# Hybrid decoder trunk on one core: the shared-sum adds placed behind the next step, the loads at pair ends redistributed, and six seven-product steps in the last pair

## The chip, the cores and the metric

The kernel runs on one core of one Trainium2 chip. The metric is device time in microseconds (us) of one execution; lower is better. Before the change three executions took 1211.99, 1211.93 and 1210.82 us, median 1211.93.

## What is computed

One decoder layer on 272 positions (16 meta tokens and 256 tokens) of width 2048: retention heads and mLSTM heads share an input projection `w_in` and an output projection `w_out`; a gated feed-forward network with a causal convolution of width 3 follows; all in float32.

```python
u  = rmsnorm(h, norm_ffn)
up = causal_dwconv(u @ w_up, ffn_conv_w, ffn_conv_b)     # w_up: 2048 x 11264
gate, val = jnp.split(up, [FFN_DIM], axis=-1)            # FFN_DIM 5632
h  = h + (jax.nn.silu(gate) * val) @ w_down              # w_down: 5632 x 2048
return rmsnorm(h, norm_final)[:, N_META:]
```

The change touches the last line but one (the down-projection) and, in small things, how weight tiles are loaded everywhere.

## The kernel before

**Precision.** A product in float32 is made of three matmuls. Each weight tile is loaded raw, ScalarE copies it to a rounded type (`whi`), VectorE subtracts that from the raw tile (`wlo`), and TensorE adds hi by hi, lo-activation by hi, and hi-activation by `wlo` in PSUM (L141, L143, L150 to L153; in the down-projection L768, L770, L821 to L824, L846 to L849). `whi` and `wlo` have five buffers each.

**Raw tiles.** `raw_home` gives them from two names, `wraw0` and `wraw1`, two buffers each. `load_raw` counts loads and takes the sides in the rhythm 0, 0, 1, 1; a tile's load waits until the reader of the tile that last had its buffer is done. Nearly all loads are issued by SyncE (SP), whose queue is in order: a load that waits holds up those behind it. DMAs that accumulate are issued by GpSimd (POOL), also in order.

**The feed-forward part** runs in two halves of the hidden width. In each, an up-projection (88 half-tile loads `in_wu`) is followed by a down-projection into 4 column blocks of 512, taken as two pairs, `b = 0` and `b = 2`. Each pair walks through 11 steps `q` of 256 hidden channels (2 row tiles `tt`, 2 column blocks `j`). A plain step has 24 matmuls of 512 columns. A *seven step* (`seven`, q = 1 to 8) makes seven products instead of eight in Winograd's manner, 21 matmuls: the combined activations `sh`, `sl` are ready, the combined weights are made of a raw tile of four quarters (`left[0]` or `left[1]`, name `hT`, 1 MB), a difference `ta` that VectorE makes (L832, into `wraw`), and a sum `tb` that was formed in DRAM (`Early`: accumulating DMAs during the projections, paced by a count of loads; result `kept`, loaded by POOL, L930). The products that only one block needs go to `cs` (PSUM name `atps`), those that several blocks need to `ps` (`mmps`).

**Ends of pairs.** After the last seven step, `share` gives the shared sums to the residual `hn` with four accumulating DMAs (`onto`, L865). After the last plain step ScalarE copies each `cs` out (L1003) into one of the tiles `x`, which become free when an `onto` has landed, and VectorE adds it to `hn` (L1004), for which the `onto` of the same block must have landed. The first splits of the next pair are placed behind the last copy (`emptied`).

**The last pair** (half 1, `b = 2`, `final`) takes q = 0, 1, 6, 2, 7, 3, 4, 5, 8, 9, 10; the q of `BOTH` (6, 7, 8) are plain there, the others of 1 to 8 seven steps. Its last four plain q (`alone`) do column block 2 first; block 3 follows at the end, row tile 0 in full width, row tile 1 in two halves of 256 columns, so that the final norm of tile 0 (`finish`, L728 to L744) runs beside the products of tile 1. `times_gain` multiplies finished blocks by the final gain on GpSimd (L715) during the seven steps of the last pair.

**Order.** Each engine's order is fixed when the program is built: a scheduler with a model of times places the instructions, under `issue_after` (place behind) and `high_priority`. A change in one place can so change the order in another.

## Time and profile before

| | |
|---|---|
| median of three executions | 1211.93 us |
| profiled execution | 1212.01 us |
| its span, first to last instruction | 1210.2 us (1.8 us around it) |
| PE busy / DVE busy / ACT busy / POOL busy | 99% / 79% / 59% / 21% of the span |
| mean granted TensorE clock | 0.998 |
| memory read and written | 268.59 MB and 42.47 MB, 257 GB/s over the span |

PE is TensorE, DVE VectorE, ACT ScalarE, POOL GpSimd. Down-projection of half 0: 718 to 774 us (`b = 0`) and 774 to 836 us (`b = 2`); of half 1: 1087 to 1145 and 1145 to 1202, then the tail to 1210.2. Busy shares average over stages, so a stage is read by its own window; matmuls are pipelined, so a row of one shows 0.39 us while the next starts 0.23 us later, and a loss is read from start to start.

### The profile page before, as it was taken

Reading aid. Unit: us, or ns where it says so; the run is one execution under the profiler, and the core shown is the slowest. Engines: PE = TensorE matmul, PEld = TensorE weight load, DVE = VectorE, ACT = ScalarE, POOL = GpSimd, SP = SyncE. Lnnn points to the kernel's source line nnn. Section 1 sums busy time; section 2 is a strip of 40 time slices with the busy share of each in tenths; the row PEclk is TensorE's granted clock in tenths of the full one; section 3 lists DMA queues with packets and bytes.
Section 4 is the critical chain, followed back from the end, with each engine's and each line's share of the span. In section 5 each row is a group of like instructions: output and inputs, shape, how many; then the busy total and the mean of one; then the engine's idle time right before and its main releaser. Section 6 shows DMA issues by size and latency. Waiting matters only on the chain.

```text
span 1210.2 us, 23069 instructions
## 1 busy us (share of the span) xinstructions
PE 1198.8 (99%) x8947; PEld 1150.3 (95%) x8947; DVE 951.6 (79%) x1390; ACT 713.4 (59%) x973; POOL 258.7 (21%) x349
## 2 busy tenths in 40 slices
PE   9999999999999999999999999999999999999997
PEld 9999999999999999999999998878999999998786
DVE  8877778766775867788889779897877777778896
ACT  8657746656556556555555557665655555556673
POOL 0100022223231322233132100101133223300132
PEclk9999999999999999999999999999999999999999
DMA  7765677878786977788887757777888778847955
GB/s 278 263 224 159 203 235 210 254 217 238 209 244 208 260 223 222 238 256 227 237 229 224 233 181 261 229 249 228 271 228 252 240 222 237 221 161 265 291 195 183
DMA packets 102366, 278.50 MB, mean 230 GB/s; under 512 B 16432, under 2 KB 20656, under 8 KB 102128
## 3 DMA queue, kind: packets, MB, share of 16 engines
q1 hardware_dynamic: 84016, 239.06, 58.0%
q0 software_dynamic: 17664, 37.11, 17.5%
q8 instruction: 70, 1.15, 0.4%
q10 hardware_dynamic: 576, 0.85, 0.2%
q14 instruction: 40, 0.33, 0.1%
HBM read 268.59 MB, written 42.47 MB: 257 GB/s over the span
## 4 chain that ended last, share of the span: by engine, by line
PE 95%; DMA 2%; DVE 1%; ACT 0%; issue 0%; SPq 0%; DVEq 0%; ACTq 0%
PE mmps L150 25%; PE mmps L153 25%; PE mmps L151 25%; PE atps L821 2%; PE mmps L849 2%; PE atps L822 2%; PE atps L824 2%; PE mmps L846 2%; PE mmps L847 2%; PE atps L846 1%; PE atps L847 1%; PE atps L849 1%; DMA wraw<-in_wu 1%; DVE wlo L770 1%; DMA hT<-kept 1%; PE atps L444 1%
## 5 line engine op out<-in xcount | busy, mean ns | idle before, releaser
L141 ACT CAST whi<-wraw 128x1024 fp32r<-128x1024 f32 x346 | 361.8, 1049 | 334.0 <-PE mmps L151 221.6
L143 DVE TENSOR_TENSOR wlo<-wraw,whi 128x1024 fp32r<-128x1024 f32 x346 | 430.2, 1246 | 79.0 <-ACT whi L141 74.8
L150 PE MATMUL mmps<-uh,whi 128*128 128x258 f32 x1408 | 345.3, 283 | 0.6 <-ACT whi L141 0.6
L151 PE MATMUL mmps<-ul,whi 128*128 128x258 f32 x1408 | 345.0, 281 | 0.0
L151 PEld LDWEIGHTS mmps<-ul,whi 128*128 128x128 f32 x1408 | 266.6, 189 | 0.1
L150 PEld LDWEIGHTS mmps<-uh,whi 128*128 128x128 f32 x1408 | 265.3, 188 | 0.9 <-ACT whi L141 0.8
L150 PE MATMUL mmps<-xh,whi 128*128 128x272 f32 (+2 forms) x864 | 219.7, 287 | 0.0
L151 PE MATMUL mmps<-xl,whi 128*128 128x272 f32 (+2 forms) x864 | 218.2, 285 | 0.0
L153 PE MATMUL mmps<-uh,wlo 128*128 128x258 f32 x1408 | 197.9, 283 | 0.0
L153 PEld LDWEIGHTS mmps<-uh,wlo 128*128 128x128 f32 x1408 | 181.7, 189 | 0.0
L151 PEld LDWEIGHTS mmps<-xl,whi 128*128 128x128 f32 x864 | 162.6, 188 | 0.0
L150 PEld LDWEIGHTS mmps<-xh,whi 128*128 128x128 f32 x864 | 162.5, 188 | 0.1
L210 POOL TENSOR_TENSOR pace<-whi 128x1 f32<-128x1 f32 x87 | 52.2, 600 | 429.9 <-ACT whi L141 411.8
L153 PE MATMUL mmps<-xh,wlo 128*128 128x272 f32 (+2 forms) x864 | 126.8, 285 | 0.0
L153 PEld LDWEIGHTS mmps<-xh,wlo 128*128 128x128 f32 x864 | 114.5, 188 | 0.0
L697 DVE TENSOR_TENSOR cu<-mmps,rstd 128x258 f32<-128x258 f32 x88 | 37.6, 427 | 72.9 <-PE mmps L153 72.2
L770 DVE TENSOR_TENSOR wlo<-hT,whi 128x1024 fp32r<-128x1024 f32 x58 | 69.3, 1218 | 3.5 <-ACT whi L768 3.5
L768 ACT CAST whi<-hT 128x1024 fp32r<-128x1024 f32 x58 | 59.3, 1049 | 15.7 <-DMA hT<-kept 5.3
L768 ACT CAST whi<-wraw 128x1024 fp32r<-128x1024 f32 (+1 forms) x58 | 46.6, 835 | 35.5 <-DVE wraw L832 17.7
L151 PE MATMUL mmps<-mixl,whi 128*128 128x258 f32 x256 | 63.1, 283 | 0.0
L150 PE MATMUL mmps<-mixh,whi 128*128 128x258 f32 x256 | 62.5, 283 | 0.0
L770 DVE TENSOR_TENSOR wlo<-wraw,whi 128x1024 fp32r<-128x1024 f32 (+1 forms) x58 | 53.2, 952 | 1.5 <-ACT whi L768 0.5
(272 smaller groups left out, 1768.3 us busy)
## 6 DMA issues: line engine op xcount, KB each, us to landing
wraw<-in_wu SPq DMA_DIRECT2D x176, 512.0 KB, 4.5
wraw<-in_wi SPq DMA_DIRECT2D x108, 512.0 KB, 4.5
wraw<-in_wo SPq DMA_DIRECT2D x32, 512.0 KB, 5.4
wraw<-in_wd SPq DMA_DIRECT2D x30, 512.0 KB, 5.6
kept<-in_wd SPq DMA_DIRECT2D x29, 512.0 KB, 6.8
kept<-in_wd POOLq DMA_DIRECT2D x58, 256.0 KB, 6.7
hT<-in_wd SPq DMA_DIRECT2D x29, 512.0 KB, 4.9
kept<-kept POOLq DMA_DIRECT2D x29, 256.0 KB, 5.4
```

The lines of the kernel that those rows point to most:

```text
L141: nc.scalar.copy(hi, raw)
L143: nc.vector.tensor_tensor(out=lo, in0=raw, in1=hi.bitcast(F32), op=ALU.subtract)
L150: nc.tensor.matmul(ps, hi[:, k, :], xh(kk), start=kk == first, stop=False)
L151: nc.tensor.matmul(ps, hi[:, k, :], xl(kk), start=False, stop=False)
L153: nc.tensor.matmul(ps, lo[:, k, :], xh(kk), start=False, stop=kk == last)
L210: with tc.issue_after(nc.gpsimd.tensor_tensor(out=pace, in0=x, in1=x, op=ALU.add).ins):
L697: evacuated = nc.vector.tensor_tensor(out=u, in0=ps[:, :NQ], in1=rstd2, op=ALU.mult)
L768: copied = nc.scalar.copy(hi, x)
L770: return copied, nc.vector.tensor_tensor(out=lo, in0=x, in1=hi.bitcast(F32), op=ALU.subtract)
L846: nc.tensor.matmul(o, sh[:, f, m, :], hi[:, i, :], start=begin, stop=False)
L847: nc.tensor.matmul(o, sl[:, f, m, :], hi[:, i, :], start=False, stop=False)
L849: nc.tensor.matmul(o, sh[:, f, m, :], lo[:, i, :], start=False, stop=end)
```

## The change

Six things change. The j = 1 adds of pair `b = 0` (L1004 before, L1019 now) are put into a list `later` and issued behind the last split of the next pair's first seven step. `BOTH` shrinks to q = 7, 8: step 6 of the last pair is a seven step, the order of its steps is 0, 1, 2, 7, 3, 4, 5, 6, 8, 9, 10, one more unit is formed by `Early` (30, not 29, from load 36 on, not 40), and the parked activations `a21` are two tiles, not three. The load of step 2 of pair `b = 2` goes from SP's queue to POOL's, behind `share`. The load of the final gain `gfin` (1 MB) is cut into four, issued during steps 3 to 6 of pair `b = 0` of half 1. The plain loads of the last pair follow its new steps. `loads` starts at 3, which shifts the rhythm of the raw sides by three everywhere.

```diff
@@ -35,7 +35,7 @@
 WARM = 8
-AHEAD, AHEAD_STEP, REST, RESUME = 40, 22, 222, 238
+AHEAD, AHEAD_STEP, REST, RESUME = 36, 22, 222, 238
@@ -114,7 +114,8 @@
     last_load = None
-    loads = paced = 0
+    loads, paced = 3, 0
     def raw_home(shape, side):
         return wpool.tile(shape, F32, name=f"wraw{side}", bufs=2)
@@ -189,7 +190,7 @@
     FAST = [1, 2, 3, 4, 5, 6, 7, 8]
     PLAIN = [q for q in range(NQD) if q not in FAST]
-    BOTH = FAST[-3:]
+    BOTH = FAST[-2:]
     class Early:
@@ -841,7 +842,7 @@
                 lo = wpool.tile([P, 2, 512], F32R, name="wlo", bufs=5)
                 n = len(to)
                 with tc.issue_after(after.ins) if first and after else nullcontext():
-                    copied, _ = split(hi[:, :n, :], lo[:, :n, :], w)
+                    copied, parted = split(hi[:, :n, :], lo[:, :n, :], w)
                 for i, (m, o, begin, _) in enumerate(to):
                     nc.tensor.matmul(o, sh[:, f, m, :], hi[:, i, :], start=begin, stop=False)
                     nc.tensor.matmul(o, sl[:, f, m, :], hi[:, i, :], start=False, stop=False)
@@ -856,6 +857,7 @@
                 with tc.issue_after(reached.ins):
                     for tt, _, c0, c1 in norm:
                         times_gain(tt, c0, c1)
+            return parted
         def block(tt, b):
             return hn[:, tt, b * 512 : (b + 1) * 512]
@@ -893,7 +895,6 @@
             more_cm = pool("more", 2, side="right")
             more = more_cm.__enter__()
             gfin = more.tile([P, DM], F32, name="gfin", bufs=1)
-            nc.gpsimd.dma_start(gfin, io["gfin"])
             junk = more.tile([P, 512], F32, name="junk", bufs=1)
             kept21 = more.tile([P, 2, len(BOTH), P], F32R, name="a21", bufs=1)
             nc.scalar.copy(kept21, left[1].rearrange("p a n -> p (a n)")[:, 0 : 2 * len(BOTH) * P].rearrange("p (s f n) -> p s f n", s=2, n=P))
@@ -901,7 +902,7 @@
         homes, raws = {}, {}
-        begun = shared = None
+        begun = shared = summed = None
         def load(to, src):
             nonlocal begun
@@ -918,23 +919,30 @@
             nonlocal turn
             raw = left[turn]
             turn = 1 - turn
-            load(raw[:, 2:4, :], io["wd7"][b // 2, half * NQD + q][:, 2:4, :])
-            load(raw[:, 1, :], io["wd7"][b // 2, half * NQD + q][:, 1, :])
-            load(raw[:, 0, :], early[b, half * NQD + q].kept[:, 0, :])
+            w = io["wd7"][b // 2, half * NQD + q]
+            parts = ((raw[:, 2:4, :], w[:, 2:4, :]), (raw[:, 1, :], w[:, 1, :]), (raw[:, 0, :], early[b, half * NQD + q].kept[:, 0, :]))
+            for to, src in parts:
+                if (b, q) == (2, 2):
+                    with tc.issue_after(shared.ins):
+                        nc.gpsimd.dma_start(to, src)
+                else:
+                    load(to, src)
             homes[b, q] = raw
         def load_sum(b, q):
+            nonlocal summed
             tb = sums_home[1][:, FAST.index(q) % 2, :][:, None, :]
             with tc.issue_after(shared.ins) if shared else nullcontext():
-                nc.gpsimd.dma_start(tb[:, 0, :], early[b, half * NQD + q].kept[:, 1, :])
+                summed = nc.gpsimd.dma_start(tb[:, 0, :], early[b, half * NQD + q].kept[:, 1, :])
             homes[b, q] = homes[b, q], sums_home[0], tb
         def split_step(raw, to=wpool):
             return split_w(raw, [P, 2, 512], to)
         lag = 4
-        gains = []
+        gains, later = [], []
         emptied = None
         for b in (0, 2):
             cs = {}
@@ -944,7 +952,7 @@
             ps = [mm.tile([P, 512], F32, name="mmps") for _ in range(4)]
             final = half == 1 and b == 2
-            steps = [0, 1, 6, 2, 7, 3, 4, 5, 8, 9, 10] if final else range(NQD)
+            steps = [0, 1, 2, 7, 3, 4, 5, 6, 8, 9, 10] if final else range(NQD)
             fast = [q for q in steps if q in FAST and not (final and q in BOTH)]
             plain = [q for q in steps if q not in fast]
             alone = plain[-lag:] if final else []
@@ -960,7 +968,12 @@
                     due = []
                     if final and q != fast[0]:
                         due, gains = gains[:1], gains[1:]
-                    seven(b, q, cs, ps, q == fast[0], q == fast[-1], emptied, due)
+                    done = seven(b, q, cs, ps, q == fast[0], q == fast[-1], emptied, due)
+                    if q == fast[0]:
+                        with tc.issue_after(done.ins):
+                            while later:
+                                later.pop(0)()
                     if q == fast[-1]:
                         with tc.high_priority() if final else nullcontext():
                             shared = share(ps, b, final)
@@ -972,12 +985,10 @@
                 if final:
                     if q == 0:
-                        load_plain(b, 6, 0)
-                    elif q == 6:
                         load_plain(b, 7, 0, 1)
-                    elif q in (3, 4, 5):
-                        load_plain(b, q + 5, 0 if q < 5 else 1, 1)
-                    if q in (1, 2, 3):
+                    elif q in (4, 5, 6):
+                        load_plain(b, q + 4, 0 if q < 6 else 1, 1)
+                    if q in range(1, 5):
                         load_seven(b, q + 2)
                         load_sum(b, q + 2)
                 else:
@@ -988,6 +999,10 @@
                         load_sum(b, q + 2)
                     if q == 8:
                         load_plain(b, 10, 1)
+                    if (half, b) == (1, 0) and q in range(3, 7):
+                        cols = slice((q - 3) * 512, (q - 2) * 512)
+                        with tc.issue_after(summed.ins):
+                            nc.gpsimd.dma_start(gfin[:, cols], io["gfin"][:, cols])
                     if b == 0:
                         if q == 7:
                             load_seven(2, 1)
@@ -1001,7 +1016,9 @@
                         x = x_tile((4, 3, 1, 0)[2 * j + n])
                         emptied = nc.scalar.copy(x, cs[tt, j])
-                        nc.vector.tensor_tensor(out=block(tt, b + j), in0=block(tt, b + j), in1=x, op=ALU.add)
+                        later.append(lambda to=block(tt, b + j), x=x: nc.vector.tensor_tensor(out=to, in0=to, in1=x, op=ALU.add))
+                        if j == 0 or b == 2:
+                            later.pop(0)()
                         if half == 1:
                             gains.append((tt, b + j, c, c + 512))
                     elif j == 0:
```

VectorE where the last pair begins. L143/L144 split a plain tile, L832/L833 make `ta`, L770/L771 split the parts of a seven step. Before:

```order
L143 TENSOR_TENSOR wlo<-wraw_13666,whi 128x1024
L1004 TENSOR_TENSOR hn<-hn,x_5926 128x512 x4
L770 TENSOR_TENSOR wlo<-hT,whi 128x1024 x2
L770 TENSOR_TENSOR wlo<-wraw_13719,whi 128x1024
L770 TENSOR_TENSOR wlo<-wraw_13720,whi 128x512
L832 TENSOR_TENSOR wraw_13719<-hT 128x1024
L143 TENSOR_TENSOR wlo<-wraw_13755,whi 128x1024
```

The same place now:

```order
L144 TENSOR_TENSOR wlo<-wraw_13675,whi 128x1024
L1019 TENSOR_TENSOR hn<-hn,x_5931 128x512 x2
L771 TENSOR_TENSOR wlo<-hT,whi 128x1024 x2
L771 TENSOR_TENSOR wlo<-wraw_13726,whi 128x1024
L771 TENSOR_TENSOR wlo<-wraw_13727,whi 128x512
L1019 TENSOR_TENSOR hn<-hn,x_5931 128x512 x2
L833 TENSOR_TENSOR wraw_13726<-hT 128x1024
```

Two of the four adds moved behind the splits of step 1; step 2 follows them directly, since step 6 no longer stands between.

SP where the second up-projection begins (`in_wd` with `wraw1`: the two tiles of the last plain step; the `in_wu` tiles are needed in the order of their numbers). Before:

```order
L909 DMA wraw1_9990<-in_wd 128x1024
L909 DMA wraw1_9992<-in_wd 128x1024
L127 DMA wraw0_10071<-in_wu 128x1024
L127 DMA wraw0_10162<-in_wu 128x1024
L127 DMA wraw1_10101<-in_wu 128x1024
L127 DMA wraw1_10132<-in_wu 128x1024
```

The same place now:

```order
L910 DMA wraw1_9995<-in_wd 128x1024
L910 DMA wraw1_9997<-in_wd 128x1024
L128 DMA wraw0_10076<-in_wu 128x1024
L128 DMA wraw0_10106<-in_wu 128x1024
L128 DMA wraw1_10137<-in_wu 128x1024
L128 DMA wraw1_10167<-in_wu 128x1024
```

The tile needed second had the buffer that the last plain step leaves; now it has the other buffer of side 0, and the tile needed third has that one.

PE near the end, from the pair of matmuls that completes row tile 0 (`wlo,mh 128x512 x2`) on. Before:

```order
L824 MATMUL atps<-wlo,mh 128x512 x2
L824 MATMUL atps<-wlo,a_13228 128x256
L824 MATMUL atps<-wlo,sh 128x256
L821 MATMUL atps<-whi,a_13228 128x256
L822 MATMUL atps<-whi,a_13228 128x256
L821 MATMUL atps<-whi,sh 128x256
L822 MATMUL atps<-whi,sl 128x256
```

The same place now:

```order
L825 MATMUL atps<-wlo,mh 128x512 x2
L823 MATMUL atps<-whi,ml 128x256
L825 MATMUL atps<-wlo,mh 128x256 x2
L822 MATMUL atps<-whi,a_13233 128x256
L823 MATMUL atps<-whi,a_13233 128x256
L822 MATMUL atps<-whi,sh 128x256
L823 MATMUL atps<-whi,sl 128x256
```

The pair now stands later among the 256-column matmuls of row tile 1: before, 44 of these followed it to the end of PE's program, now 27.

## Rows read from the trace of the kernel before

**Rows 1.** Chain of waits: shares of the span by engine
```profile
PE 95%; DMA 2%; DVE 1%; ACT 0%; issue 0%; SPq 0%; DVEq 0%; ACTq 0%
```
**Rows 2.** Window of the last pair's seven steps: PE, PEld, DVE, ACT, POOL busy
```profile
1145.00:1184.00 39.00, 39.00 (x169) 31.36 (x169) 36.87 (x33) 26.84 (x35) 12.24 (x11) 1.00 0.61 210
```
**Rows 3.** Timeline of PE, half 1: a seven step's start and the next's
```profile
1092.81 0.39 PE L846 MATMUL atps<-whi,sh 128*128 128x512 f32 x1
...
1097.71 0.39 PE L846 MATMUL atps<-whi,sh 128*128 128x512 f32 x1
```
**Rows 4.** Timeline of PE: where it waits in the down-projections
```profile
814.45 0.63 PE L849 MATMUL mmps<-wlo,sh 128*128 128x512 f32 x2
815.87 0.51 PE L846 MATMUL atps<-whi,sh 128*128 128x512 f32 x1 [0.79 <-ACT whi L768]
...
818.56 0.51 PE L846 MATMUL mmps<-whi,sh 128*128 128x512 f32 x1 [0.16 <-ACT whi L768]
...
836.54 0.39 PE L150 MATMUL mmps<-uh,whi 128*128 128x258 f32 x1 [0.56 <-ACT whi L141]
...
1129.78 0.50 PE L846 MATMUL mmps<-whi,sh 128*128 128x512 f32 x1 [0.18 <-ACT whi L768]
```
**Rows 5.** Chain of waits, the step ahead of 836.54
```profile
826.73 8.63 DMA wraw<-in_wu
```
**Rows 6.** Timeline of DVE, half 0, b = 2
```profile
776.24 0.69 DVE L1004 TENSOR_TENSOR hn<-hn,x 128x512 f32<-128x512 f32 x1 [0.82 <-DMA hn<-x]
778.27 0.69 DVE L1004 TENSOR_TENSOR hn<-hn,x 128x512 f32<-128x512 f32 x1 [1.34 <-DMA hn<-x]
...
816.12 1.23 DVE L832 TENSOR_TENSOR wraw<-hT 128x1024 f32<-128x1024 f32 x1 [1.82 <-DMA hT<-kept]
```
**Rows 7.** Timeline of DVE, last pair
```profile
1148.65 2.36 DVE L770 TENSOR_TENSOR wlo<-hT,whi 128x1024 fp32r<-128x1024 f32 x2
1150.92 1.82 DVE L770 TENSOR_TENSOR wlo<-wraw,whi 128x1024 fp32r<-128x1024 f32 x2
1152.65 1.22 DVE L832 TENSOR_TENSOR wraw<-hT 128x1024 f32<-128x1024 f32 x1
1153.79 2.35 DVE L143 TENSOR_TENSOR wlo<-wraw,whi 128x1024 fp32r<-128x1024 f32 x2
...
1159.59 2.36 DVE L832 TENSOR_TENSOR wraw<-hT 128x1024 f32<-128x1024 f32 x1
...
1180.10 3.44 DVE L143 TENSOR_TENSOR wlo<-wraw,whi 128x1024 fp32r<-128x1024 f32 x2
```
**Rows 8.** Timeline of POOL, last pair
```profile
1159.57 1.30 POOL L715 TENSOR_TENSOR hn<-hn,gfin 128x512 f32<-128x512 f32 x1
```
**Rows 9.** Timeline of ACT, where the last pair begins
```profile
1146.38 2.00 ACT L768 CAST whi<-hT 128x1024 fp32r<-128x1024 f32 x2
```
**Rows 10.** Timeline of PE, last pair: last lo of `ta`
```profile
1181.65 0.63 PE L849 MATMUL mmps<-wlo,sh 128*128 128x512 f32 x2
```
**Rows 11.** DMA issues 1134 to 1137 us: KB, median us to landing
```profile
hT<-kept SPq DMA_DIRECT2D x1, 256.0 KB, 13.0
```
**Rows 12.** DMA issues 1139 to 1141 us
```profile
wraw<-kept POOLq DMA_DIRECT2D x2, 256.0 KB, 10.6
```
**Rows 13.** Timeline of POOL, issues ahead of the last pair
```profile
1139.07 1.79 POOL L930 DMA_DIRECT2D wraw<-kept  x2
```
**Rows 14.** Timeline of PE, tail
```profile
1196.35 0.63 PE L824 MATMUL atps<-wlo,mh 128*128 128x512 f32 x2
...
1201.81 0.40 PE L824 MATMUL atps<-wlo,mh 128*128 128x256 f32 x2
```
**Rows 15.** Timeline of DVE, tail
```profile
1197.02 0.69 DVE L888 TENSOR_TENSOR hn<-atps,hn 128x512 f32<-128x512 f32 x1 [0.67 <-PE atps L824]
...
1201.94 0.14 DVE L720 TENSOR_REDUCE rest<-ss 128x1 f32<-128x4 f32 x1
...
1202.25 0.42 DVE L888 TENSOR_TENSOR hn<-atps,hn 128x256 f32<-128x256 f32 x1
```

## The prediction, made before the changed kernel was run

> **What bounds the kernel now.** I read the chain of waits first: 95% of the span is PE, and nothing else has more than 2% [rows 1]. So the end is PE's own work plus the few places where PE waits, plus the tail behind PE's last matmul. Second, the rows of PE with a wait in brackets. In the down-projections the larger ones are four [rows 4]. Measured from start to start they cost more than the bracket says: the pair that starts at 814.45 takes 2 x 0.233 = 0.47, the next matmul starts at 815.87, so 0.95 is lost where the bracket has 0.79. With the same 0.16 added to each: 0.95 and 0.32 in pair b = 2 of half 0, 0.72 at the start of the second up-projection, 0.34 in pair b = 0 of half 1; together 2.3 us. Third, the window of the last pair's seven steps: PE works through all 39 us, but DVE is busy for 36.87 of them, 95% [rows 2]. There DVE is the second limit, a little below PE. Fourth, the tail.
>
> **The change part by part.** All sums stand against the profiled execution, 1212.01 us (span 1210.2 and 1.8 around it), which is 0.08 above the median of the runs.
>
> *Products of the last pair.* A seven step is 21 matmuls in 4.90 us [rows 3], 0.233 each. Step 6 goes from 24 to 21: 3 x 0.233 = **-0.70**. PE is gapless there, so this counts, if VectorE keeps up (below).
>
> *The loads at the start of the second up-projection.* PE stops at 836.54 for a tile whose load was on its way for 8.63 us from 826.73 [rows 4, 5]. That tile, needed second, had to wait for the buffer of the last plain step; by the new order it takes a buffer that comes free a step earlier, and the tile needed third, 2.8 us later, takes the old place. I count all of it: **-0.72** (bounds 0 and -0.72; a load that is issued sooner can only be slowed by others in flight). Elsewhere the new rhythm moves loads under a PE that doesn't wait; I cost it at nothing, bounds -0.1 and +0.3, by the next smallest wait, 0.32.
>
> *Adds behind the next step, half 0.* VectorE waits 0.82 and 1.34 us for the accumulating DMAs ahead of its j = 1 adds [rows 6]; the first splits of the next pair stand behind them. They now come first. The two adds themselves (0.6 each when back to back) still come before step 2, so that what VectorE is ahead by there is only the waits, 2.16, less what the splits wait for ScalarE's last copy, about 1. Later in the same pair VectorE waits for a load again, 1.82 us at 816.12 [rows 6]: the load waits for a buffer that VectorE frees, so being ahead is handed on in part. Of the 0.95 + 0.32 I take a third: **-0.40** (bounds -1.27, all of it, and +0.9, if step 2's load comes late, see the rival).
>
> *gfin in four, and the smaller parked tile, half 1, b = 0.* The 1 MB load no longer stands beside the pair's first loads, but its pieces stand between the loads of steps 5 to 8. **-0.25** of the 0.34 lost there (bounds -0.34, and +0.5, about one more wait of the size seen).
>
> *One more unit of Early* adds a 512 KB load and three DMAs of 256 KB in stretches where none of PE's larger waits lies: nothing, bounds 0 and +0.3.
>
> *VectorE in the last pair.* Now its account. Before, step 1's splits start at 1148.65 and VectorE works without a gap until plain step 8's splits at 1180.10 [rows 7]. From those rows: the splits of a seven step take 2.27 + 1.73 = 4.0; `ta` 1.2 alone, and 2.3 when GpSimd multiplies beside it [rows 7, 8]; a plain split 1.17. Before: 4.0 + 1.15 + 2 x 1.17 (plain 6) + 4.0 + 1.17 (plain 7) + 3 x (2.3 + 4.0) = 31.6, and 1148.65 + 31.6 = 1180.2: the account is right to 0.1. After: the splits can start when ScalarE has its first copy of step 1, 1146.38 + 1.05 = 1147.4 [rows 9], perhaps 0.5 earlier, since the accumulations for which the copies wait share the queues with less; I take 1146.9. Then 4.0, two adds 1.2, `ta` 1.2, 4.0, plain 7 1.15, three times 2.3 + 4.0, and for step 6 2.3, 2.27 and 1.17 to the lo of `ta`: 1146.9 + 36.2 = 1183.1. PE wanted the lo of the last seven step's `ta` at 1181.65 [rows 10]; it will want that of step 6 0.70 sooner for the fewer products, and 0.93 later since four matmuls of step 8 now stand ahead of it: 1181.9. So VectorE, which had some 2 us in hand, is late by 1.2: **+1.20** (bounds 0, if splits start near 1145.5, and +2.5, if it is GpSimd beside every `ta` and no start gained). A seven step costs VectorE 6.3 beside GpSimd, against PE's 4.90; a plain step 2.3 against 5.6. That is why the sixth one uses up the reserve. The gains upstream shift PE and VectorE alike and change nothing here.
>
> *The tail.* Row tile 0 of the last block is complete with the pair at 1196.35, that is at 1196.82; 42 matmuls of 256 columns lie between this and 1201.81, so one takes (1201.81 - 1196.82) / 42 = 0.119 [rows 14]. Before, 44 of these follow: 5.2 us, PE's end at 1202.05. VectorE starts the add of tile 0 at 1197.02, 0.2 after the pair, and its chain for tile 0 (sum of squares, root, scaling) reaches the next free place at 1201.94; its very last add follows at 1202.25, 0.2 behind PE's end: the two just meet [rows 15]. In the changed order 27 follow the pair, 3.2 us, while the chain for tile 0 is as long as it was, 4.9, and still stands ahead of the last add on VectorE. (The 0.42 us add of tile 1's first half leaves that chain, and a square of as many columns stands on ScalarE's part of it; I set them equal.) So the last add starts 0.2 + 4.9 = 5.1 after the pair, where PE is ready 0.2 + 3.2 = 3.4 after it: **+1.70** (bounds +1.2, if the two L720, L721 that moved ahead shorten the chain more, and +2.2, if ScalarE's square lengthens it). From the last add to the end, 7.95 us before, nothing changes.
>
> *The load of step 2, pair b = 2, on POOL's queue.* Issued at 1135.71 by SP it took 13.0 us before [rows 11]. On POOL's queue it stands behind four accumulations, where the sums stand now, issued at about 1139.1 [rows 13] and landing 10.6 later [rows 12]. Three DMAs ahead of the sums: the last about 1140.2, landing at 1150.8 by the sums' row, 1153.2 by the 13.0. VectorE wants it at 1146.9 + 4.0 + 1.2 = 1152.1. I take the sums' row, the same queue and the same moment: no cost; the other end is +1.1.
>
> Sum: -0.70 - 0.72 - 0.40 - 0.25 + 1.20 + 1.70 = +0.83, so 1212.84 for a profiled run, **1212.8** for the median.
>
> **The rivals.**
>
> *A, the waits go and no new one comes.* If VectorE's reserve holds (splits at 1145.5 or GpSimd's multiplications falling elsewhere), all four waits vanish, and the tail order costs nothing: -0.70 - 0.72 - 1.27 - 0.34 = -3.0, 1208.9. For it: the waits ahead of the adds are real [rows 6]. Against it: the account of VectorE, exact for before, and the counts 44 and 27, which are fixed in the program.
>
> *B, slower: the moved load lands late.* POOL's issues, 0.9 us each [rows 13], come after `share`, so the load of step 2 starts some 4.5 us later than before. If it takes 13.0 again, it lands at 1153.2 and VectorE, which has no reserve, hands the 1.1 on to PE; in half 0 the same delay comes at the start of b = 2 and turns -0.40 into +0.9 (the bound above). 0.83 + 1.1 + 1.3 = +3.2, **1215.2**. It decides from a landing later than 1152. The Trainium skill, "DMA: Bandwidth & Descriptors", section "Issuing engines are not separate DMA queues", says that DMAs of all engines end up on the same 16 DMA engines, and a second issuer only saves issue time; by that the load moves later by as much as its issue does, and B follows. The same page, section "SWDGE vs HWDGE vs iDMA", has each DMA engine take turns between what GpSimd and what the hardware queues bring, by which POOL's queue would have its own share. The trace has 10.6 on POOL's queue beside 13.0 on SP's at the same moment [rows 11, 12], which is nearer to the second; no run here separates them yet.
>
> *C, the change doesn't do what it says:* ScalarE's copies hold the splits as long as the adds did, so nothing of the start is gained: VectorE starts at 1147.9, +1.0 on the account, and the half 0 waits stay, +0.4: 1212.84 + 1.4 = 1214.2.
>
> *D, VectorE keeps up in the last pair*, but the tail is as I say: 0.83 - 1.20 = -0.37, 1211.6.
>
> **How the numbers follow.** Repeated runs stand 1.2 us apart, and 0.2% is 2.4 us: about what a measurement can tell from no change. Forecast 0.45 (own range 1211.9 to 1213.9), D 0.23, C 0.12, A 0.09, B 0.11. Faster by over 2.4 us (below 1209.5) needs A: 0.09. Slower (above 1214.4) needs B or the upper part of C: 0.14. The rest, 0.77, is no change that can be told. The range 1209.8 to 1215.0 leaves out A's lower and B's upper half.
>
> **What would show it.** In the changed profile: (1) the wait of PE for `whi` at the start of the second up-projection is gone; (2) VectorE is gapless from step 1's splits to step 8's, and PE shows a wait for `wlo` (or for `whi` behind it) of about a microsecond near 1180 in the last seven step; (3) the last 256-column add of VectorE starts some 1.9 us behind PE's last matmul, with L738's successor just ahead of it; (4) the hT load of step 2 lands before VectorE asks. The prediction is wrong where VectorE has idle time in the last pair with PE gapless (D, A), where the last add follows PE's end at once, or where VectorE waits for the moved load (B).

## The result and the profile after

The changed kernel takes 1215.28 us, median of seven runs (1214.55 to 1216.87), against 1211.62 of seven runs of the kernel before: ratio 1.0034, 95% interval 1.0023 to 1.0046. That is 0.34% slower, clear of the noise, and 0.28 us outside the range of the prediction.

The profiled execution has a span of 1213.5 us, 3.27 more than before. Set matmul against matmul, the two traces part as follows:

| stretch | after minus before, us | forecast |
|---|---|---|
| up to the last pair's first seven step | -2.27 (and +0.17 from the first microseconds of the program) | -1.37 |
| products of the last pair | -0.70 | -0.70 |
| waits of PE in the last pair's seven steps, with the slow first matmul behind each | +2.89 | +1.20 |
| waits of PE in the plain steps behind them | +1.04 | 0 |
| start of PE's last matmul to start of VectorE's last add (1.94, before 0.32) | +1.62 | +1.70 |
| last add to the end | +0.48 | 0 |

The rows add up to 3.23; the other 0.04 is not assigned.

The waits, in the timeline of PE after (start, duration, operation, in brackets the idle time and who ended it):

```profile
1141.67 0.50 PE L822 MATMUL atps<-whi,mh 128*128 128x512 f32 x1 [0.60 <-ACT x L1018]
...
1164.82 0.50 PE L847 MATMUL atps<-whi,sh 128*128 128x512 f32 x1 [0.47 <-ACT whi L769]
...
1174.85 0.50 PE L847 MATMUL mmps<-whi,sh 128*128 128x512 f32 x1 [1.55 <-ACT whi L769]
```

Of the waits of before [rows 4], those at 815.87, 836.54 and 1129.78 are gone, that at 818.56 has its like at 817.1; the one at 1141.67 is new, and so are the two in the last pair, where PE had worked without a gap [rows 2]. What stands around the first of these two, GpSimd after:

```profile
1153.99 9.09 POOL L856 TENSOR_TENSOR junk<-wraw 128x1 f32<-128x1 f32 x1 [3.89 <-ACT junk L712]
1163.04 1.29 POOL L716 TENSOR_TENSOR hn<-hn,gfin 128x512 f32<-128x512 f32 x1
1164.28 0.56 POOL L938 DMA_DIRECT2D wraw<-kept  x1
1164.86 0.21 POOL L856 TENSOR_TENSOR junk<-wraw 128x1 f32<-128x1 f32 x1
```

VectorE after, in the same time:

```profile
1160.07 1.82 DVE L771 TENSOR_TENSOR wlo<-wraw,whi 128x1024 fp32r<-128x1024 f32 x2
1161.81 1.22 DVE L833 TENSOR_TENSOR wraw<-hT 128x1024 f32<-128x1024 f32 x1
1164.80 3.73 DVE L771 TENSOR_TENSOR wlo<-hT,whi 128x1024 fp32r<-128x1024 f32 x2 [1.78 <-ACT whi L769]
```

ScalarE after:

```profile
1163.11 0.63 ACT L712 ACTIVATE junk<-hn 128x512 f32<-128x512 f32 x1 [3.55 <-POOL junk L856]
...
1167.61 0.62 ACT L769 CAST whi<-wraw 128x512 fp32r<-128x512 f32 x1 [0.94 <-DMA wraw<-kept]
```

GpSimd's marker (an operation on one element, placed only to pace what follows; 0.21 us at 1164.86) lasts from 1153.99 to 1163.08. VectorE runs back to back all this time, each operation starting 0.08 before the last has ended, and stops for the first time at 1161.81 + 1.22 = 1163.03. Three things stand behind the marker: the multiplication, the load of a sum (issued at 1164.28, and ScalarE waits for it at 1167.61), and ScalarE's square, which writes the same scratch `junk`; behind the square stand ScalarE's casts, and for these VectorE then stops for 1.78 us. In this stretch VectorE is starved by an engine that it shuts out itself. The second, larger wait (1.95 us from start to start, up to 1174.85) is for the cast of step 5's difference `ta`. VectorE makes that `ta` behind one of the step's splits, which takes 2.31 us instead of 1.2 beside a multiplication; before, step 5's `ta` came ahead of its splits. After, then before:

```profile
1170.19 2.31 DVE L771 TENSOR_TENSOR wlo<-hT,whi 128x1024 fp32r<-128x1024 f32 x1
1172.42 1.21 DVE L833 TENSOR_TENSOR wraw<-hT 128x1024 f32<-128x1024 f32 x1
```
```profile
1173.86 2.31 DVE L832 TENSOR_TENSOR wraw<-hT 128x1024 f32<-128x1024 f32 x1
1176.09 2.35 DVE L770 TENSOR_TENSOR wlo<-hT,whi 128x1024 fp32r<-128x1024 f32 x2
```

The tail after, PE and VectorE [rows 14, 15]:

```profile
1199.56 0.63 PE L825 MATMUL atps<-wlo,mh 128*128 128x512 f32 x2
...
1202.99 0.40 PE L825 MATMUL atps<-wlo,mh 128*128 128x256 f32 x2
```
```profile
1200.22 1.02 DVE L890 TENSOR_TENSOR hn<-atps,hn 128x512 f32<-128x512 f32 x2 [1.35 <-PE atps L825]
...
1205.04 0.42 DVE L890 TENSOR_TENSOR hn<-atps,hn 128x256 f32<-128x256 f32 x1
```

From the pair that completes row tile 0 to VectorE's last add it is 1205.04 - 1200.03 = 5.0 us (5.4 before), and PE is done 3.2 after the pair, as the counts had it. The tail's loads come late besides: issued 1184 to 1189 us, they take 7.3 us in the median (DMA issues), against 5.0 for the four of before (1182 to 1187 us). I take it that VectorE frees the buffers later and that the last accumulations are then on the queues too; no run varied this alone.

```profile
wraw<-in_wd SPq DMA_DIRECT2D x4, 512.0 KB, 7.3
```

### The profile page after: what moved, and what is told of

Read it like the earlier page. It is cut to its first block, busy times and chain, and to the rows that moved or that the text cites. A ratio compares the mean times of both kernels' runs of the same rounds, so it can differ in the third digit from the quotient of the medians.

```text
span 1213.5 us, 23080 instructions
## 1 busy us (share of the span) xinstructions
PE 1198.8 (99%) x8944; PEld 1149.4 (95%) x8944; DVE 951.9 (78%) x1392; ACT 713.8 (59%) x974; POOL 271.3 (22%) x365
## 4 chain that ended last, share of the span: by engine, by line
PE 93%; DMA 2%; DVE 2%; issue 1%; ACT 1%; POOL 1%; SPq 0%; DVEq 0%; ACTq 0%; POOLq 0%
PE mmps L151 25%; PE mmps L154 25%; PE mmps L152 25%; PE mmps L847 2%; PE mmps L848 2%; PE mmps L850 2%; PE atps L825 1%; PE atps L822 1%; PE atps L847 1%; PE atps L823 1%; PE atps L850 1%; PE atps L848 1%; DMA hn<-x 1%; DMA hT<-kept 1%; POOL junk L856 1%
## 5 line engine op out<-in xcount | busy, mean ns | idle before, releaser
L144 DVE TENSOR_TENSOR wlo<-wraw,whi 128x1024 fp32r<-128x1024 f32 x344 | 426.0, 1240 | 78.7 <-ACT whi L142 73.3
L771 DVE TENSOR_TENSOR wlo<-hT,whi 128x1024 fp32r<-128x1024 f32 x60 | 75.3, 1278 | 6.3 <-ACT whi L769 6.2
L771 DVE TENSOR_TENSOR wlo<-wraw,whi 128x1024 fp32r<-128x1024 f32 (+1 forms) x60 | 55.1, 952 | 2.6 <-ACT whi L769 1.4
```

The costliest lines, as they stand in the source:

```text
L144: nc.vector.tensor_tensor(out=lo, in0=raw, in1=hi.bitcast(F32), op=ALU.subtract)
L771: return copied, nc.vector.tensor_tensor(out=lo, in0=x, in1=hi.bitcast(F32), op=ALU.subtract)
```

## The experiments

Ratios are to runs of the kernel before on the same chip; five rounds each.

**1. A scratch of its own for the marker**

```diff
-                reached = nc.gpsimd.tensor_tensor(out=junk[:, 0:1], in0=tb[:, 0, 0:1], ...)
+                reached = nc.gpsimd.tensor_tensor(out=mark, in0=tb[:, 0, 0:1], ...)
```

> The changed kernel, with GpSimd's pacing marker (L856) written into a tile of its own instead of the scratch column that ScalarE's squares also write. Theory 1 (starved marker): the marker waits 9 us for a gap in VectorE's work, ScalarE's next square waits for it through the shared scratch, and the casts behind the square starve VectorE; with a scratch of its own PE's wait at 1163.95 (0.74 us with its restart) goes and the one at 1172.90 (1.97 us) falls below 0.7, and the tail's loads come about 2 us earlier, so that the tail's waits (1.0) mostly go: 3 us less than the changed kernel, about 1212.3. Theory 2 (VectorE's account of the prediction): VectorE has too much to do in the last pair whatever ScalarE waits for; PE still loses 1.2 us or more there and the time falls by less than 1 us, to 1214.3 or above.

Measured 1215.74 us, ratio 1.0031 (1.0021 to 1.0041): no gain. In its profiled execution, the fastest of its nine (1213.18), the marker was let in after 1.1 us at most and ScalarE never waited for it, yet PE still lost 2.7 us in the last pair. GpSimd, VectorE and PE of this run:

```profile
1151.89 1.14 POOL L856 TENSOR_TENSOR mark<-wraw 128x1 f32<-128x1 f32 x1 [2.66 <-DMA wraw<-kept]
1153.09 2.19 POOL L716 TENSOR_TENSOR hn<-hn,gfin 128x512 f32<-128x512 f32 x1
```
```profile
1150.63 2.35 DVE L771 TENSOR_TENSOR wlo<-hT,whi 128x1024 fp32r<-128x1024 f32 x2
1152.90 2.93 DVE L771 TENSOR_TENSOR wlo<-wraw,whi 128x1024 fp32r<-128x1024 f32 x2
```
```profile
1172.94 0.50 PE L847 MATMUL mmps<-whi,sh 128*128 128x512 f32 x1 [1.52 <-ACT whi L769]
...
1178.20 0.50 PE L847 MATMUL mmps<-whi,sh 128*128 128x512 f32 x1 [0.54 <-ACT whi L769]
```

GpSimd got in although VectorE left no gap, and each of its four multiplications made a VectorE operation 1.1 us longer (2.93 for two that take 1.82 alone). So neither the shared scratch nor a marker that is shut out for long is needed for the loss: VectorE's own work beside GpSimd is enough, which is theory 2 of the expectation. (The median says no more than that nothing was gained; the trace is of one execution.)

**2. No marker, no multiplications in the seven steps**

```diff
-                reached = nc.gpsimd.tensor_tensor(...)
-                with tc.issue_after(reached.ins):
-                    for tt, _, c0, c1 in norm:
-                        times_gain(tt, c0, c1)
```

> The changed kernel without the marker and without GpSimd's four multiplications by the final gain during the last pair's seven steps (the computation leaves out these multiplications; the squares stay). Theory 1: as with the marker's own scratch, no more: VectorE loses the four stretches of 1.1 us beside GpSimd only where it has reserve, about 1212.3. Theory 2: VectorE is the limit, and the 4 x 1.1 us that its operations last longer beside GpSimd are what makes it late; without them PE's waits in the last pair all go: 3.9 us less, about 1211.4, and clearly (over 0.8 us) below the kernel with the marker's own scratch.

This kernel leaves the four multiplications out altogether. Measured 1211.71, ratio 1.0004 (0.9995 to 1.0013): the slowdown is gone. Windows of the last pair, after and in this run (columns as in [rows 2]):

```profile
1147.00:1183.00 36.00, 33.97 (x144) 26.23 (x143) 33.16 (x31) 23.96 (x33) 19.37 (x13) 1.00 0.51 171
```
```profile
1147.00:1183.00 36.00, 36.00 (x156) 28.97 (x155) 34.47 (x36) 25.04 (x34) 3.96 (x6) 1.00 0.63 210
```

PE is gapless again, and VectorE gets 36 instructions done in the time of 31. VectorE alone can feed six seven steps; it can't beside GpSimd.

**3. Five seven steps, the rest of the change kept** (`BOTH = FAST[-3:]`, the old order of steps and loads)

> The changed kernel with five seven-product steps in the last pair again (step 6 plain, the old order of steps and loads), all else of the change kept. Both theories: products 0.70 more, and PE's waits of the last pair (2.9 in the steps, 1.0 in the tail) go, with the order of the tail before (44 matmuls of 256 columns behind the pair that completes row tile 0), 2.1 less there: 1215.28 + 0.70 - 3.9 - 2.1 = 1210.0. If the moved adds and loads themselves are what hurts at the last pair, it stays at 1213 or above.

Measured 1210.62, ratio 0.9994 (0.9985 to 1.0003): near the expected 1210.0, and no different from the kernel before.

**4. The sixth seven step alone, on the kernel before** (`BOTH = FAST[-2:]` and what follows from it)

> The kernel before with nothing changed but the sixth seven-product step in the last pair (its order of steps, loads and one more unit formed early); adds, queues, gfin and the rhythm of loads stay. By VectorE's account of the prediction the splits of step 1 start at 1148.65 as before, so VectorE is later by 36.2 - 31.6 = 4.6 us than before at the end of step 6, against 2 us in hand; with products -0.70 and the tail (36 matmuls behind row tile 0 here, so +0.6): slower than before by 3 to 6 us, about 1215, no better than the whole change. If instead the moved adds and loads made the trouble, it is within 1 us of before.

Measured 1214.81, ratio 1.0033 (1.0020 to 1.0045): the whole slowdown, with the adds, queues, rhythm and `gfin` as they were. PE loses 3.5 us in the seven steps of its profiled execution. Its GpSimd shows the same long wait:

```profile
1153.20 9.08 POOL L855 TENSOR_TENSOR junk<-wraw 128x1 f32<-128x1 f32 x1 [2.69 <-ACT junk L711]
```

**5. The marker alone left out** (the multiplications stay, each behind its square)

> The changed kernel without GpSimd's marker alone: the four multiplications by the gain stay in the last pair's seven steps, each placed behind ScalarE's square of its block. Of the 3.6 us that leaving out marker and multiplications gave back, this separates the two. If the marker that waits 9 us for VectorE to pause, with the load of a sum queued behind it on GpSimd and ScalarE's square behind it, is most of it: 1212 to 1213. If the multiplications beside VectorE (4 x 1.1 us) are: a multiplication now waits for a pause as the marker did, or holds VectorE as before, and PE's waits in the last pair stay at 2 us or more: 1214.5 to 1216.

Measured 1219.58, ratio 1.0068 (1.0055 to 1.0082): worse than either case expected. GpSimd and VectorE of this run:

```profile
1153.98 13.60 POOL L716 TENSOR_TENSOR hn<-hn,gfin 128x512 f32<-128x512 f32 x1 [3.89 <-ACT junk L712]
1167.52 0.56 POOL L936 DMA_DIRECT2D wraw<-kept  x1
```
```profile
1165.21 1.21 DVE L771 TENSOR_TENSOR wlo<-wraw,whi 128x1024 fp32r<-128x1024 f32 x1
1173.37 0.69 DVE L771 TENSOR_TENSOR wlo<-wraw,whi 128x512 fp32r<-128x512 f32 x1 [6.95 <-ACT whi L769]
```

Now nothing stops ScalarE, so VectorE runs on without a pause until 1166.4, and the multiplication waits for it 12.4 us of its 13.6. The load of the sum stands behind it in GpSimd's queue; VectorE stops because that sum isn't there, and only then is GpSimd let in, to issue the load that VectorE waits for. PE loses 5.6 us in one piece.

**6. As 5, the sums from step 3 on loaded through SP's queue**

```diff
-                summed = nc.gpsimd.dma_start(tb[:, 0, :], early[...].kept[:, 1, :])
+                load(tb[:, 0, :], early[...].kept[:, 1, :])     # half 1, b = 2, q > 2
```

> The run without the marker (1219.6, ratio 1.0068, where a multiplication on GpSimd waited 13.6 us for VectorE and the load of a sum stood behind it), with one more change: the last pair's sums from step 3 on are loaded through SP's queue. If the loss comes from what stands behind the waiting GpSimd, PE's wait of 5.6 us goes, however long the multiplication waits, and the time falls by 5 us or more, to 1212 to 1214. If the waiting itself is harmless and the 4 x 1.1 us beside VectorE are the loss, it falls by less than 3 us.

Measured 1213.16, ratio 1.0019 (1.0010 to 1.0028), 6.4 us below run 5 (5.9 by the ratios). The profiled execution is the slowest of its eleven (1216.11). GpSimd's four multiplications, the first of which now waits longer still, and VectorE where they are let in:

```profile
1156.63 23.75 POOL L716 TENSOR_TENSOR hn<-hn,gfin 128x512 f32<-128x512 f32 x4 [14.34 <-ACT junk L712]
```
```profile
1173.14 3.89 DVE L771 TENSOR_TENSOR wlo<-wraw,whi 128x1024 fp32r<-128x1024 f32 x2
```

VectorE's operations keep their length up to 1173.14, so no multiplication has run before then: 16 us of waiting cost nothing once nothing stands behind GpSimd. What is left in the seven steps, 1.17 us from start to start ahead of 1180.47 in this execution (1.7 with the slower single matmuls), I take as the price of the multiplications themselves (3.89 here instead of 1.82).

**7. As 6, with the tail's order** (42 matmuls of 256 columns held behind the pair that completes row tile 0)

> As the run before, with 42 instead of 27 of the 256-column matmuls behind the pair that completes row tile 0; all is computed. From the last add's distance to PE's end (1.9 us in the changed kernel, 0.3 to 0.5 with 42 to 44) 1.0 to 1.5 us less than the run before: about 1211.5, ratio 1.0005; a version that loses nothing against the kernel before but gains nothing either.

Measured 1212.46, ratio 1.0013 (1.0004 to 1.0022): nearer, 0.7 us less, not the 1.0 to 1.5. The last add starts 0.51 after PE's last matmul, from 1.93.

**8 and 9. The multiplications moved behind the last accumulations; the same with the tail's order**

```diff
+                        with tc.issue_after(shared.ins):
+                            for tt, _, c0, c1 in put:
+                                times_gain(tt, c0, c1)
```

> The changed kernel with GpSimd's four multiplications by the final gain moved from the last pair's seven steps to behind its last accumulations, where VectorE has idle time; no marker is needed then. All is computed. If those multiplications beside VectorE are what made PE wait (4 x 1.1 us), this keeps the gain of leaving them out, 1211.7, within 0.7; if they only matter wherever they stand, or delay the final norm, 1213 or more.

> As the run before, and 42 instead of 27 of the 256-column matmuls of row tile 1 held behind the pair that completes row tile 0. If the last add of VectorE is bound by tile 0's chain, as the prediction's tail has it, it then falls to 0.1 us behind PE's end, from 1.8, and the time falls by 1.0 to 1.7 us against the run before, to about 1210.3 (less the more PE has to wait for the last load without work to fill the wait). If that order costs nothing, the two are equal.

Measured 1214.77, ratio 1.0026 (1.0015 to 1.0037), and 1212.76, ratio 1.0018 (1.0009 to 1.0026). PE no longer waits in the seven steps, but the first expectation failed. VectorE and GpSimd of run 8:

```profile
1184.97 5.65 DVE L878 TENSOR_TENSOR hn<-hn,x 128x512 f32<-128x512 f32 x1
```
```profile
1184.68 5.38 POOL L716 TENSOR_TENSOR hn<-hn,gfin 128x512 f32<-128x512 f32 x4
```

Here GpSimd was first, and four of its operations in a row shut VectorE out: an add of 0.7 us took 5.65, the tail's splits came late, and PE waited 1.2. The tail's order (run 9) gave back 2.0 us by the medians and by the profiled executions, 1.0 by the ratios, about the difference expected, though not the 1210.3; the last add starts 0.51 after PE's last matmul instead of 1.93.

**10. Multiplications within VectorE's final scaling, and the tail's order**

```diff
-            if c0 >= late:
+            if c0 >= late or c0 < 1024:
```

> The changed kernel with GpSimd's four multiplications by the gain taken out of the last pair and done within VectorE's final scaling (one operation with two factors in place of one), and with 42 matmuls of 256 columns behind the pair that completes row tile 0. All is computed. From the run without those multiplications (ratio 1.0004): -1.4 for the tail's order, +0.45 for the slower scaling of 1024 columns in the last chain: about 1210.2 where before has 1210.9, ratio 0.9994 to 1.000. If the waits return, 1.002.

Measured 1210.94, ratio 1.0003 (0.9994 to 1.0012). With GpSimd out of the way and the tail's order mended, six seven steps and all of the computation cost as much as the kernel before, and no less.

**11. The four adds ahead of the next step, as before the change**

> The changed kernel with one part undone: all four adds of pair b = 0 ahead of the next pair's first splits again, as before the change. If the moved adds put the last pair in trouble (theirs are 1.2 us of VectorE behind step 1), PE's waits in the last pair fall by about 1.2 us, 1214. If VectorE's account holds, the adds cost the same 1.2 us in either place and the waits ahead of them (2.2 us in half 0, 1.6 in half 1) come back on top: the pair b = 2 of half 0 loses about 1 us more than in the changed kernel (0.3), the last pair as much as now or more: 1215.3 to 1217.

Measured 1213.07, ratio 1.0018 (1.0009 to 1.0027): 1.9 us better than the change by the ratios, where I expected no gain. The order of the tail moved with the edit (37 matmuls behind the pair): in the profiled executions, 2.2 us apart, the last add starts 0.58 after PE's last matmul instead of 1.93, which is 1.35 of it, and PE loses 1.8 us in the seven steps instead of 2.9. The marker was let in after 1.07 us in the mean here. So this run doesn't tell what the adds' place is worth by itself.

**12. The load of step 2 on SP's queue**

> The changed kernel with one part undone: the load of step 2 of pair b = 2 on SP's queue again. In the changed kernel it landed at 1147.2, 3.2 us ahead of VectorE's use of it at 1150.4, so rival B of the prediction (it lands late on POOL's queue) expects nothing of the changed kernel's loss to go; if anything the accumulating DMAs, which then share the queues with 1 MB more, land later and the first splits with them: 1215 to 1216. If the POOL queue was the trouble, 1213 or below.

Measured 1217.86, ratio 1.0057 (1.0044 to 1.0071): 2.6 us worse than the change, so the move to POOL's queue is a gain. In the profiled execution PE begins the last pair's seven steps at 1150.38 instead of 1147.38; the tail's order, which moved with this edit too, gives 1.4 back. Issues from 1134 to 1137 us, in this run and after:

```profile
hT<-kept SPq DMA_DIRECT2D x1, 256.0 KB, 13.8
```
```profile
hT<-kept POOLq DMA_DIRECT2D x1, 256.0 KB, 10.3
```

**13 and 14. The rhythm of loads alone, on the kernel before; the same with a cast behind two copies**

```diff
-    loads = paced = 0
+    loads, paced = 3, 0
```

> The kernel before, with nothing changed but the count of loads starting at 3. As the prediction has it: PE's wait of 0.72 us at the start of the second up-projection goes, the waits in the pairs stay: 1211.62 - 0.72 = 1210.9. Rival: the load needed third then waits for the same buffer and PE waits there instead: 1211.6.

> The kernel before with the count of loads starting at 3 (as in an earlier run, which showed the wait of 0.72 gone and one of 0.83 where the last pair begins) and ScalarE's cast of the last pair's second plain tile placed behind its first two copies out of PSUM. If the saving was given back because that cast waits for a late load ahead of the copies that free PE's accumulators, the wait at 1141 goes and the run is 0.7 to 0.9 us below the earlier one: about 1210.5 where before has 1211.1, ratio 0.9994. If PE then waits for that tile's cast instead, nothing is gained, ratio 1.0001 as it was.

Measured 1211.62, ratio 1.0001 (0.9992 to 1.0010), and 1210.75, the same ratio and interval. In run 13 the wait at 836.54 is gone and a new one stands where the last pair begins. PE and ScalarE of this run:

```profile
1143.00 0.50 PE L821 MATMUL atps<-whi,mh 128*128 128x512 f32 x1 [0.68 <-ACT x L1003]
```
```profile
1141.41 1.05 ACT L141 CAST whi<-wraw 128x1024 fp32r<-128x1024 f32 x1 [1.91 <-DMA wraw<-in_wd]
1142.37 1.56 ACT L1003 COPY x<-atps 128x512 f32<-128x512 f32 x3
```

ScalarE stands at a cast whose load is late, with the copies that free PE's accumulators behind it. Before, those copies began at 1143.14 and PE's next step at 1143.78; a PE that comes a microsecond sooner meets them. In run 14 that wait is gone from the profile, but the ratio is the same: whether the saving is lost elsewhere can't be told at this size.

**15. Run 3 with that cast behind two copies**

> All of the change but the sixth seven-product step (as in the earlier run with five, ratio 0.9994), with the same placing of the cast behind two copies. A version meant to beat both: no wait of PE over 0.2 us in the down-projections; the earlier run's 0.1 us at 1141 and what other executions of it lose there go: ratio 0.9985 to 0.9994. If VectorE's later start of that tile's split matters, 1.000.

Measured 1211.6, ratio 1.0009 (1.0001 to 1.0018): no better than run 3, against the expectation. None of these versions beats the kernel before by more than the noise.

## Why the prediction was wrong

**The products and the tail** came as forecast: -0.70, and +1.62 from PE's last matmul to the last add for the forecast +1.70; the sign and size follow from the counts 44 and 27, and VectorE's last add starts 5.0 after the pair for the forecast 5.1. The step "from the last add to the end, nothing changes" was off by +0.48; this stretch is 7.9 to 8.5 us in most of the runs, and I have no cause for the difference.

**The start of the second up-projection, half 0 and half 1, b = 0**: -2.27 for the forecast -1.37 in this execution; all of half 0's large wait went, not a third. But as a term of the time the -0.72 was wrong: the rhythm alone nets nothing (run 13), since part of it comes back at 1141 as a wait for ScalarE's copies, which the prediction did not look for; and all parts but the sixth step together give 0.06% with an interval that holds zero (run 3). Nor can the -2.27 be put down to the parts that the forecast credits. Run 4 has the adds, the rhythm and `gfin` as before, and in its profiled execution PE has no wait above 0.13 us from half 0's down-projection to the last pair's first seven step, which starts 3.4 us sooner than before (1146.08). Which build or execution has these waits is not explained.

**The step that failed is "VectorE in the last pair", +1.20.** Its measured size is 2.89 in the seven steps; another 1.04 in the tail, which the sum had at nothing, I put down to loads that wait for VectorE's buffers, which is argued and not shown. The direction was right, and the cause too: runs 3 and 4 put the whole slowdown on the sixth seven step, and run 2 shows that it lies between VectorE and GpSimd's work beside it. What the account of VectorE had wrong can be read off the trace after, with PE's lead of 2.10 at the first seven step added. The splits of step 1 end 0.4 later than forecast (1149.18 + 2.10 against 1146.9 + 4.0), since the last of them waits 1.02 us for the sum. VectorE stands still for 1.78 us at 1163.03, which was put at nothing. GpSimd makes it 3.6 us longer instead of the forecast 4.4, since one multiplication falls into that pause. So the lo of step 6's `ta` is ready at 1182.30 + 2.10 = 1184.4 and not at 1183.1: 2.5 us after the time set for PE, where the forecast has 1.2. The waits also come earlier than the forecast "near 1180": at 1164.82 and 1174.85, for casts of steps 4 and 5.

The pause of 1.78 us came from what the account left out: I asked what stands behind each waiting instruction on VectorE, but not on GpSimd, where the loads of the sums and, by a shared scratch, ScalarE's squares stand. Runs 5 and 6 show what that can cost in their kernels: with the loads behind the waiting GpSimd PE loses 5.6 us at once, with the loads on another queue the longer wait costs nothing. But it does not explain the size by itself. In run 1 the pause is gone, VectorE needs 32.1 us from its adds to the lo of step 6's `ta` for the 32.2 of the account, and PE still loses 2.7. PE waits there for the casts of `ta` in steps 5 and 6, while the account compared the two engines at one place alone, the lo of the last `ta`, and did not look at the order within step 5. How much of the 2.7 that order makes stays open, since no run changed it alone.

The Trainium skill, "SBUF — State Buffer", section "SBUF: two separate sides", says that a VectorE instruction with two SBUF inputs and a GpSimd instruction that reads SBUF exclude each other, and whichever starts first keeps the other blocked for its whole length. The trace agrees: beside a multiplication of 1.3 us a VectorE operation takes 1.1 us longer. It shows more: the block can go on over a chain of instructions that follow each other without a gap, in either direction (16 us in run 6, 5.65 us in run 8). It need not: in run 1 (1.14 us at most), and at 1166.22 in the kernel before (0.92), the marker was let in beside a chain just as dense. What decides between the two isn't shown.

**Rival B** named the right time, 1215.2, for the wrong reason: the moved load's last part was issued at 1136.85, not at 1140.2, and landed at 1147.2, 3.2 us before VectorE took it up, and putting it back costs 2.6 us (run 12). Of the two rules weighed there the landing times, 10.3 us on POOL's queue and 13.8 on SP's, are nearer to the second, that POOL's queue has its own share. **Rivals A and D** needed a VectorE that keeps up, which it did only without GpSimd. **Rival C**, that ScalarE's copies hold the splits as the adds did, did not come: VectorE began step 1 at 1144.06, 4.6 us before its time of before, of which 2.1 is PE's own lead; at the last split of step 1 (1148.57, before 1152.05) 1.4 beyond that lead is left.

What stays open besides: how the 1.9 us of run 11 divide, and why single executions of one kernel differ by 4 to 6 us (run 8: 1211.9 to 1218.0; the kernel before on the same chip, in 27 executions: 1209.14 to 1213.24).

## What to carry to other kernels

When an engine is at its limit, ask not only whether it keeps up, but who works beside it and what stands behind whom. Here each of four GpSimd operations made VectorE 1.1 us longer, and in some stretches GpSimd was shut out for 9 to 16 us, with everything queued behind it late. So put no loads that the critical path needs into the queue of an engine that also computes in competition with the bottleneck. Compare two engines at every place where one needs the other, not only at the last. And a wait removed early counts only if the next tight place, here the copies at a pair's end, moves along with it.

## What the hardware showed that was not expected

An operation of 0.2 us on GpSimd took 9.09, one of 1.3 us 13.6, each until VectorE's first pause; an add of 0.7 us on VectorE took 5.65 behind four operations of GpSimd. In run 7 a GpSimd operation of 1.3 us took 13.60 as well, but was let in at about 1166.5 between two VectorE operations without a pause; GpSimd and VectorE of that run:

```profile
1154.16 13.60 POOL L716 TENSOR_TENSOR hn<-hn,gfin 128x512 f32<-128x512 f32 x1 [14.55 <-ACT junk L712]
```
```profile
1163.11 2.35 DVE L771 TENSOR_TENSOR wlo<-hT,whi 128x1024 fp32r<-128x1024 f32 x2
1165.38 2.92 DVE L771 TENSOR_TENSOR wlo<-wraw,whi 128x1024 fp32r<-128x1024 f32 x2
1168.23 2.31 DVE L771 TENSOR_TENSOR wlo<-hT,whi 128x1024 fp32r<-128x1024 f32 x1
```

After each wait of PE in the profile after, its next matmul took 0.10 to 0.11 us more than the 0.233. After the long wait of run 5 the granted clock was 0.53 from 1173 to 1177 us (near the lower of the two levels, 1.2 GHz), and a matmul took 0.43 us instead of 0.23:

```profile
1168.00:1173.00 5.00, 0.00 (x0) 0.00 (x0) 0.00 (x0) 0.28 (x1) 1.85 (x3) 0.70 0.81 298
1173.00:1177.00 4.00, 3.61 (x9) 2.85 (x10) 2.77 (x3) 2.84 (x5) 1.79 (x2) 0.53 0.09 28
```
